# The odd mixer's convolution: one product for each sixteenth of the TensorE array, straight from the gated channels

## The chip, the cores and the metric

The kernel runs on one core of a Trainium2 chip. The metric is the device time in microseconds (us) of one execution. Three runs of the kernel before took 995.54, 997.87 and 1000.76 us, with a median of 997.87 us. The engines are named as in the profile: PE is TensorE's matmul side and PEld its weight loads, DVE is VectorE, ACT is ScalarE, POOL is GpSimd, SP is the queue that issues the loads of the weights.

## The reference, cut to what matters

The program is one inference step of a two-layer decoder trunk for 256 prompt tokens and 8 single sample tokens (264 columns in all). Each layer is a SwiGLU, a mixer and a second SwiGLU, each behind an RMS norm. The change is in layer 1's mixer, the odd one, and there in the depthwise convolution over 31 positions of each of 512 channels:

```
p = h @ w_in                                   # 1024 -> 512 + 512 + 512
a, gt, xp = jnp.split(p, ODD_SPLITS, axis=-1)
glu = a * jax.nn.sigmoid(gt)
gpad = jnp.concatenate([conv_buf, glu], axis=1)
conv = lax.conv_general_dilated(gpad, conv_w[:, None, :], (1,), 'VALID',
                                feature_group_count=CONV_WIDTH) + conv_b
out_c = jax.nn.silu(layernorm(conv, ln_g, ln_b))       # over the 512 channels
pooled = ...                                           # sums of 2, 4, 8 or 16 tokens of xp
out_d = einsum('btgc,gcd->btgd', pooled, pool_w) * pool_scale
y = jnp.concatenate([out_c, out_d], axis=-1) @ w_out
```

The layer norm needs all 512 convolved channels before any of them can go on to `w_out`.

## The kernel before, in words

Everything lies with channels on the 128 partitions and the 264 tokens along the free axis, so the 1024 model channels are 8 tiles. A matmul with a weight matrix is done in three products of 128x128 by 128x264: high part of the weights with high and low part of the activations, low part of the weights with the high part. Weights come in chunks of 8 tiles of 128x128 (`raw`, loaded by SP); ACT makes the high part (`hi`), DVE the low part (`lo`).

The code is a planner: it emits instructions while it keeps an estimated clock of PE, with costs written in the helpers (`quarter` at L319, for example) and small generators that run between the products of the weight matrices when what they need is due. The order it finds is the order in which each engine executes; every engine works through its own instructions in that order and waits on semaphores for the others.

The odd mixer (`odd_mixer`, L1331) runs like this. `odd_in_cols` (L78) lists twelve column blocks of `w_in`: first `POOL_FIRST` (two) of the four pooling blocks, then for each of four channel blocks i its `a` and its gate, then the other pooling blocks. A column block is 24 products on PE (`odin_c`). `evac` (L1450) takes it out of PSUM: DVE scales `a` to `ga`, the gate to `gt`, ACT makes the sigmoid `sg`, and DVE multiplies both into `gp[i]`, the gated channels with 30 zeros ahead of them.

The convolution of block i needs 31 shifted copies of `gp[i]`. Before, `shifts` (L1359) wrote `gp[i]` to DRAM (`gd[i]`, L1362) and read it back four times (L1368) in another layout, `rr`: a group of 32 partitions holds the same 32 channels, shifted by 0, 1, 2 or 3 tokens, and along the free axis stand the four groups of channels. Then `conv` (L1386) ran 8 steps of 4 products, each 128 rows deep and 32 columns wide (L322, `quarter`): the 128 rows are 4 taps of 32 channels, the weights `dg` a diagonal matrix for each tap, and the four products of a step stand in different column groups of the array. The result is one PSUM bank, which ACT takes to `cv[i]` with the bias.

Behind the convolutions follow the steps of the layer norm, each a short exchange of PE with DVE and ACT: `mean` (L1487) gives `mu` (a product with a constant matrix that averages over channels), four subtractions, four squares `csq`, their sum, `cvar`, an inverse square root on DVE (`cvv` to `cv_y`), `cvb` (spread over the partitions), four scalings `cn`, the SiLU `cs`, and the split into `oyh` and `oyl` (the parts `y0` to `y3`). Meanwhile PE runs the output projection `od_o` (`mixer_out`, L793): for six of the eight output blocks first the rows that come from the pooling channels (k = 7, 6, 5, 4), 72 products, then those from the convolution (k = 0 to 3), then the last two blocks. The pooling channels come from `pooled` (L1409, DVE) and `pool_mm` (L1438, a product `pp` on PE, split by ACT and DVE).

`side` (L1560) makes the diagonal matrices `dg` on DVE, beside the two SwiGLUs ahead of the odd mixer.

Of the kernel before, what the change touches and what calls it, by code (L numbers as in the profile page):

```python
# [20 lines left out]
P = 128  # L21
D = 1024
KT = D // P
SEQ = 256
# [50 lines left out]
POOL_FIRST = 2  # L75
# [52 lines left out]
TAPS, QUADS = 31, 8  # L128
WIN = 4 * (QUADS - 1) + SEQ
# [53 lines left out]
def trunk(ctx, tc, a, o):  # L183
# [68 lines left out]
    locks = {"s1": [0.0] * 2, "s2": [0.0], "mm": [0.0] * 4, "rr": [0.0] * 4, "pool": [0.0], "big": [0.0] * 6,   # L252
# [1078 lines left out]
    def odd_mixer(src, next_g, dg):  # L1331
        with ExitStack() as on:
            od, od2, odd = pool(on, "od"), pool(on, "od2", 2), pool(on, "odd", space=DRAM)
            gp = [od.tile([P, 32 + SEQ], F32, name=f"gp{i}") for i in range(4)]
            gd = [odd.tile([P, 32 + SEQ], F32, name=f"gd{i}") for i in range(4)]
# [18 lines left out]
            keep, shifted, pds = {}, {}, {}  # L1354

            TO_DRAM, SHIFT = 3500.0, 10600.0
            late = []

            def shifts(i):  # L1359

                yield from need(f"glu{i}")
                tc.keep_in_program_order(nc.gpsimd.dma_start(gd[i], gp[i]))  # L1362
                t = Clock.now
                yield from acquire("rr")
                yield from until(t + TO_DRAM)
                rr = shifted[i] = od2.tile([P, 4, WIN], F32, tag="rr", name=f"rr{i}", bufs=4)
                for s in range(4):
                    tc.keep_in_program_order(nc.gpsimd.dma_start(  # L1368
                        rr[32 * s:32 * s + 32], gd[i].rearrange("(j c) t -> c j t", c=32)[:, :, s:s + WIN]))
                arrive(rr, t + SHIFT)  # L1370
                produce(f"shift{i}", t + SHIFT)
                produce(f"asked{i}")

            def outputs():

                yield from need("asked3")
                n = 0
                while n < 10:
                    if late:
                        out, src = late.pop(0)  # L1380
                        tc.keep_in_program_order(nc.gpsimd.dma_start(out, src))
                        n += 1
                    else:
                        yield 50.0

            def conv(i):  # L1386

                yield from need(f"shift{i}", "glu_in")
# [10 lines left out]
                release("s2", t)  # L1399
                produce(f"cd{i}", t)  # L1400
# [49 lines left out]
            def evac(ci, ps):  # L1450
                rb = cur["rb"]
                ci -= POOL_FIRST
                if 0 <= ci < 8:
# [7 lines left out]
                    else:  # L1461
# [8 lines left out]
                        if i == 3:  # L1470
                            produce("glu_in")
# [69 lines left out]
            spawn(*[shifts(i) for i in range(4)], outputs(), mean(), *[pool_mm(i) for i in (3, 2, 1, 0)],  # L1541
# [11 lines left out]
    with ExitStack() as on:  # L1553
        dgp = pool(on, "dg")
        cw = dgp.tile([P, 4 * QUADS * 4 + 32], F32, name="cw")
        nc.gpsimd.dma_start(cw, a["convw"])
        n = QUADS * 4
        dg = [dgp.tile([P, QUADS, 4, 32], F32, name=f"dg{i}") for i in range(4)]

        def side():  # L1560

            yield 5000.0
            eye = cw[:, 4 * n:].unsqueeze(1).to_broadcast([P, 16, 32])
            for i in range(4):
                for q in range(0, QUADS, 4):
                    yield 3500.0
                    w = cw[:, i * n + 4 * q:i * n + 4 * q + 16].unsqueeze(2).to_broadcast([P, 16, 32])
                    yield from do("dve", lambda: V.tensor_mul(dg[i][:, q:q + 4].rearrange("p q j c -> p (q j) c"), eye, w))
# [6 lines left out]
        odd_mixer("ff10n", V_NG + 40, dg)  # L1575
# [45 lines left out]
def pack_inputs(inp):  # L1621
# [11 lines left out]
    def cols(v):  # L1633
# [17 lines left out]
    taps = np.zeros((4 * QUADS, 4, 4, 32), np.float32)  # L1651
    taps[:TAPS] = f["od_conv_w"][0].reshape(TAPS, 4, 4, 32)
    taps = taps.reshape(QUADS, 4, 4, 4, 32).transpose(1, 4, 2, 0, 3).reshape(P, 4 * QUADS * 4)
    convw = np.concatenate([taps, np.tile(np.eye(32, dtype=np.float32), (4, 1))], axis=1)
# [15 lines left out]
        "convw": convw,  # L1670
# [46 lines left out]
```

## Time and profile before

| what | value |
|---|---|
| median of three runs | 997.87 us (995.54 to 1000.76) |
| the profiled execution, its own time | 998.99 us |
| span of the profiled execution, first to last instruction | 997.2 us |
| mean granted TensorE clock | 0.995 |
| PE busy | 981.4 us (98%) |
| DVE, ACT, POOL busy | 659.8, 479.0, 41.3 us |
| odd mixer on PE, first product to the first one of the next SwiGLU | 703.45 to 793.23 us |

A profile is one execution. The page gives busy times and shares for the span, the span in 40 slices, and the chain of work that ended last. The trace behind it can be asked for the instructions of an engine in order of time (its timeline), for busy times in given stretches, and for the chain in order of time. A product of 128x264 is listed with some 0.28 us, but such products overlap: the next one starts 0.12 us later. A product of float32 operands stands in the trace as two pairs of a weight load and a matmul.

### The profile page before, as it was taken

How to read it: one execution, taken by the hardware profiler on the slowest of the kernel's cores; microseconds unless marked ns; L12 is line 12 of the kernel's file. 1: busy time of each engine (PE TensorE's matmuls, PEld its weight loads, DVE VectorE, ACT ScalarE, POOL GpSimd, SP SyncE). 2: the span in 40 equal slices, each digit the busy share in tenths (PEclk: the TensorE clock that was granted, in tenths of full speed). 3: DMA queues.
4: the chain of work that ended last, by engine and by line, in shares of the span. 5: the costliest groups of instructions: out<-in, count | busy, mean ns of one | idle time of the engine just before them, and what ended most of it. 6: DMA issues, size and time to landing. Idle time of an engine off the chain costs nothing.

```text
span 997.2 us, 20229 instructions
## 1 busy us (share of the span) xinstructions
PE 981.4 (98%) x8332; PEld 961.0 (96%) x8332; DVE 659.8 (66%) x1081; ACT 479.0 (48%) x718; POOL 41.3 (4%) x99
## 2 busy tenths in 40 slices
PE   9999999999999999999999999999998999999997
PEld 7999999999999999999999999999986999999996
DVE  7766666669889866665666666666863776666552
ACT  6544444465566444444444444444432754444440
POOL 2000000031000000000000000000033000000000
PEclk9999999999999999999999999999998999999999
DMA  7755555562636655555555555555583375555531
GB/s 254 256 188 181 181 189 179 181 218 95 199 125 211 218 189 175 186 176 186 178 174 177 190 181 180 190 177 183 183 250 101 107 226 181 186 185 178 188 107 44
DMA packets 50572, 178.26 MB, mean 179 GB/s; under 512 B 6167, under 2 KB 6632, under 8 KB 50480
## 3 DMA queue, kind: packets, MB, share of 16 engines
q1 hardware_dynamic: 46944, 166.38, 50.6%
q0 software_dynamic: 3248, 10.19, 3.5%
q8 instruction: 65, 1.06, 0.5%
q10 hardware_dynamic: 288, 0.41, 0.1%
q14 instruction: 27, 0.22, 0.1%
HBM read 172.94 MB, written 4.01 MB: 177 GB/s over the span
## 4 chain that ended last, share of the span: by engine, by line
PE 92%; DVE 3%; DMA 2%; issue 1%; POOL 1%; ACT 1%; SPq 0%; DVEq 0%; ACTq 0%; POOLq 0%
PE ff_c L314 50%; PE ff_o L314 26%; PE evin_c L314 6%; PE ev_o L314 2%; PE od_o L314 2%; PE odin_c L314 2%; DMA gd<-gp 1%; POOL rr L1368 1%; PE conv L322 1%; DMA rr<-gd 1%; DMA x<-in_xt 1%; DVE lo L337 1%; PE sc L314 0%; PE ff_pb L314 0%; PE fin_ss L314 0%
## 5 line engine op out<-in xcount | busy, mean ns | idle before, releaser
L337 ACT ACTIVATE hi<-raw 128x1024 fp32r<-128x1024 f32 (+1 forms) x316 | 332.0, 1051 | 405.9 <-PE ff_c L314 229.6
L337 DVE TENSOR_TENSOR lo<-raw,hi 128x1024 fp32r<-128x1024 f32 (+1 forms) x316 | 384.3, 1218 | 161.6 <-ACT hi L337 160.6
L314 PE MATMUL ff_o<-ff_gh,hi 128*128 128x264 f32 x704 | 198.4, 282 | 0.0
L314 PE MATMUL ff_o<-ff_gl,hi 128*128 128x264 f32 x704 | 198.3, 282 | 0.0
L314 PE MATMUL ff_o<-ff_gh,lo 128*128 128x264 f32 x704 | 198.3, 282 | 0.0
L314 PEld LDWEIGHTS ff_o<-ff_gh,hi 128*128 128x128 f32 x704 | 131.9, 187 | 0.0
L314 PEld LDWEIGHTS ff_o<-ff_gh,lo 128*128 128x128 f32 x704 | 131.9, 187 | 0.0
L314 PEld LDWEIGHTS ff_o<-ff_gl,hi 128*128 128x128 f32 x704 | 131.9, 187 | 0.0
L314 PE MATMUL ff_c<-start_xh,lo 128*128 128x264 f32 x352 | 99.5, 283 | 0.4 <-DVE lo L337 0.4
L314 PE MATMUL ff_c<-evn_xh,hi 128*128 128x264 f32 x352 | 99.9, 284 | 0.0
L314 PE MATMUL ff_c<-start_xl,hi 128*128 128x264 f32 x352 | 99.5, 283 | 0.4 <-DVE start_xl L337 0.3
L314 PE MATMUL ff_c<-evn_xl,hi 128*128 128x264 f32 x352 | 99.7, 283 | 0.0
L314 PE MATMUL ff_c<-evn_xh,lo 128*128 128x264 f32 x352 | 99.7, 283 | 0.0
L314 PE MATMUL ff_c<-start_xh,hi 128*128 128x264 f32 x352 | 99.5, 283 | 0.1
L314 PE MATMUL ff_c<-ff01n_xh,hi 128*128 128x264 f32 x352 | 99.2, 282 | 0.0
L314 PE MATMUL ff_c<-odn_xh,hi 128*128 128x264 f32 x352 | 99.1, 282 | 0.0
L314 PE MATMUL ff_c<-ff01n_xl,hi 128*128 128x264 f32 x352 | 98.9, 281 | 0.0
L314 PE MATMUL ff_c<-ff01n_xh,lo 128*128 128x264 f32 x352 | 98.9, 281 | 0.0
L314 PE MATMUL ff_c<-odn_xl,hi 128*128 128x264 f32 x352 | 98.9, 281 | 0.0
L314 PE MATMUL ff_c<-odn_xh,lo 128*128 128x264 f32 x352 | 98.9, 281 | 0.0
L337 DVE TENSOR_TENSOR ff_g<-ff_c,ff_sa 128x264 f32<-128x264 f32 x88 | 38.0, 432 | 58.2 <-PE ff_c L314 58.2
L314 PEld LDWEIGHTS ff_c<-start_xh,lo 128*128 128x128 f32 x352 | 66.0, 187 | 1.2 <-DVE lo L337 1.1
(362 smaller groups left out, 1909.1 us busy)
## 6 DMA issues: line engine op xcount, KB each, us to landing
raw<-in_wts SPq DMA_DIRECT2D x309, 512.0 KB, 3.4
rr<-gd POOLq DMA_DIRECT2D x16, 142.0 KB, 4.7
raw<-in_wts SPq DMA_DIRECT2D x8, 256.0 KB, 5.9
x<-in_xt SPq DMA_DIRECT2D x4, 264.0 KB, 5.7
S<-in_sgla POOLq DMA_DIRECT2D x2, 512.0 KB, 4.7
vb<-vbd POOLq DMA_DIRECT2D x4, 256.0 KB, 5.4
out_gla_s<-S POOLq DMA_DIRECT2D x2, 512.0 KB, 4.5
mat<-in_mats POOLq DMA_DIRECT2D x1, 640.0 KB, 5.9
```

The source lines that it names most:

```text
L314: return pe_run(nc.tensor.matmul(out, lhsT=lhsT, rhs=rhs, start=start, stop=stop), out, lhsT, rhs, cost)
L322: Clock.credit -= pe_run(nc.tensor.matmul(out, lhsT=lhsT, rhs=rhs, start=start, stop=stop), out, lhsT, rhs, cost)
L337: ins = tc.keep_in_program_order(f(*args, **kw))
L1368: tc.keep_in_program_order(nc.gpsimd.dma_start(rr[32 * s:32 * s + 32], gd[i].rearrange("(j c) t -> c j t", c=32)[:, :, s:s + WIN]))
```

## The change

The convolution reads `gp[i]` where it lies. The array is used as 16 blocks of 32 rows by 32 columns. Row group j holds channels 32j to 32j+31 of the block, column group n takes the taps q+n (q = 0, 4, ..., 28); the product for (j, n) has the 32x32 diagonal matrix of one tap as weights and a window of 256 tokens of `gp[i]` that begins at that tap. The planner's cost for one is 29 ns. 31 taps times 4 row groups are 124 products. Each row group writes a PSUM bank of its own (two banks of `conv`, and `convc`, `convd`); the four column groups of a bank hold four partial sums of the same 32 channels. ACT copies the four banks to `rr` (now [128, 4, 256] in SBUF), and four products with a stack of identity matrices (`eye`) add up the partial sums into a bank `cs`, from which ACT adds the bias into `cv[i]`. The copies through DRAM, their 20 DMA issues on POOL's queue and the generator `shifts` are gone; the short outputs no longer wait for them. `POOL_FIRST` becomes 1, so that one more pooling block comes behind the gates.

```diff
-POOL_FIRST = 2
+POOL_FIRST = 1
-TAPS, QUADS = 31, 8
-WIN = 4 * (QUADS - 1) + SEQ
+TAPS = 31
...
+    def sixteenth(out, lhsT, rhs, start, stop):
+
+        Clock.credit -= pe_run(nc.tensor.matmul(out, lhsT=lhsT, rhs=rhs, start=start, stop=stop), out, lhsT, rhs, 29.0)
...
-            def shifts(i):
-
-                yield from need(f"glu{i}")
-                tc.keep_in_program_order(nc.gpsimd.dma_start(gd[i], gp[i]))
-                t = Clock.now
-                yield from acquire("rr")
-                yield from until(t + TO_DRAM)
-                rr = shifted[i] = od2.tile([P, 4, WIN], F32, tag="rr", name=f"rr{i}", bufs=4)
-                for s in range(4):
-                    tc.keep_in_program_order(nc.gpsimd.dma_start(
-                        rr[32 * s:32 * s + 32], gd[i].rearrange("(j c) t -> c j t", c=32)[:, :, s:s + WIN]))
...
             def conv(i):
 
-                yield from need(f"shift{i}", "glu_in")
+
+                yield from need(f"glu{i}")
                 yield from acquire("s2")
-                ps = ps2.tile([P, 1024], F32, tag="s2", name=f"conv{i}")
-                for q in range(QUADS):
-                    for j in range(4):
-                        quarter(ps[32 * j:32 * j + 32, 0:SEQ], dg[i][:, q, j], shifted[i][:, j, 4 * q:4 * q + SEQ],
-                                q == 0, q == QUADS - 1, j)
+                yield from acquire("s1", 2)
+                yield from acquire("rr")
+                yield from slot()
+
+                both = ps2.tile([P, 2, 512], F32, tag="s2", name=f"conv{i}")
+                ps = [both[:, 0], both[:, 1], s1_psum(f"convc{i}"), s1_psum(f"convd{i}")]
+                for q in range(0, TAPS, 4):
+                    for s in range(4):
+                        for j in range(4):
+                            n = (j + s) % 4
+                            if q + n < TAPS:
+                                r = slice(32 * j, 32 * j + 32)
+                                sixteenth(ps[j][32 * n:32 * n + 32, 0:SEQ], dg[i][r, q + n], gp[i][r, q + n:q + n + SEQ],
+                                          q == 0, q + n + 4 >= TAPS)
+                rr = od2.tile([P, 4, SEQ], F32, tag="rr", name=f"rr{i}")
+                t = yield from do("act", lambda: A.copy(rr[:, 2], ps[2][:, 0:SEQ]),
+                                  lambda: A.copy(rr[:, 3], ps[3][:, 0:SEQ]), after=Clock.now)
+                release("s1", t)
+                release("s1", t)
+                t = yield from do("act", lambda: A.copy(rr[:, 0:2], both[:, :, 0:SEQ]))
+                release("s2", t)
+                yield from until(t)
+                yield from acquire("s1")
+                yield from slot()
+                cs = s1_psum(f"cs{i}")
+                for j in range(4):
+                    quarter(cs[32 * j:32 * j + 32, 0:SEQ], eye, rr[:, j], True, True, j)
                 release("rr")
                 acc = cv[i][:, 0:SEQ]
-                t = yield from do("act", lambda: A.activation(acc, ps[:, 0:SEQ], AF.Identity,
+                t = yield from do("act", lambda: A.activation(acc, cs[:, 0:SEQ], AF.Identity,
                                                               bias=vec[:, V_CB + i:V_CB + i + 1]), after=Clock.now)
...
-            spawn(*[shifts(i) for i in range(4)], outputs(), mean(), *[pool_mm(i) for i in (3, 2, 1, 0)],
+            spawn(outputs(), mean(), *[pool_mm(i) for i in (3, 2, 1, 0)],
                   *[conv(i) for i in range(4)])
...
-        dg = [dgp.tile([P, QUADS, 4, 32], F32, name=f"dg{i}") for i in range(4)]
+        dg = [dgp.tile([P, TAPS, 32], F32, name=f"dg{i}") for i in range(4)]
```

PE, where the layer norm's mean is taken, before: the last column block of `w_in` ends, `mu` follows at once, and all of `od_o` stands behind it.

```order
L314 MATMUL odin_c_9603<-ff10n_xh_8894,lo_9381 128x264
L314 MATMUL odin_c_9603<-ff10n_xh_9051,hi_9308 128x264
L314 MATMUL odin_c_9603<-ff10n_xl_9052,hi_9308 128x264
L314 MATMUL odin_c_9603<-ff10n_xh_9051,lo_9381 128x264
L314 MATMUL mu<-cvsum,oneN 128x264
L314 MATMUL mu<-cv_9014,oneN 128x264
L314 MATMUL od_o_9729<-oyh_9032,hi_9343 128x264
L314 MATMUL od_o_9729<-oyl_9033,hi_9343 128x264
```

The same place after the change: the last sum `cs` (four products) and nine products of `od_o` stand ahead of `mu`.

```order
L321 MATMUL cs_10115<-rr_10022,eye 32x256 x4
L313 MATMUL od_o_10121<-oyh_9026,hi_9477 128x264
L313 MATMUL od_o_10121<-oyl_9027,hi_9477 128x264
L313 MATMUL od_o_10121<-oyh_9026,lo_9612 128x264
L313 MATMUL od_o_10121<-oyh_9026,hi_9477 128x264
L313 MATMUL od_o_10121<-oyl_9027,hi_9477 128x264
L313 MATMUL od_o_10121<-oyh_9026,lo_9612 128x264
L313 MATMUL od_o_10129<-oyh_9026,hi_9477 128x264
L313 MATMUL od_o_10129<-oyl_9027,hi_9477 128x264
L313 MATMUL od_o_10129<-oyh_9026,lo_9612 128x264
L313 MATMUL mu<-cvsum,oneN 128x264
L313 MATMUL mu<-cv_9008,oneN 128x264
```

Nine more `od_o` products stand just ahead of this `cs`, so that 18 of the first 72 have moved in front of `mu`. Before, the fourth convolution stood nine `odin_c` products ahead of `mu`; now 30 `odin_c` products lie between it and the first `od_o`.

ACT, around the first convolutions, before: the evacuations `cv` follow the last gate's sigmoid.

```order
L337 ACTIVATE hi_9430<-raw_9321 128x1024
L337 ACTIVATE hi_9468<-raw_9383 128x1024
L337 ACTIVATE sg_9483<-gt_9478 128x264
L337 ACTIVATE cv_9011<-conv_9496,vec 128x256
L337 ACTIVATE cv_9012<-conv_9550,vec 128x256
L337 ACTIVATE hi_9610<-raw_9409 128x1024
```

After: the copies of the first convolution's four banks follow the second gate's sigmoid, ahead of the next high parts.

```order
L340 ACTIVATE sg_9225<-gt_9217 128x264
L340 ACTIVATE hi_9258<-raw_9127 128x1024
L340 ACTIVATE sg_9253<-gt_9251 128x264
L340 COPY rr_9404<-convc_9278 128x256
L340 COPY rr_9404<-convd_9279 128x256
L340 COPY rr_9404<-conv_9277 128x512
L340 ACTIVATE hi_9431<-raw_9140 128x1024
L340 ACTIVATE cv_9005<-cs_9461,vec 128x256
```

What moved: the first convolution now stands between the second and the third gate, and ACT waits for it, with the splits of the weights queued behind.

## Rows read from the trace of the kernel before

**Rows 1.** The page: busy time by engine; chain that ended last, by engine.

```profile
PE 981.4 (98%) x8332; PEld 961.0 (96%) x8332; DVE 659.8 (66%) x1081; ACT 479.0 (48%) x718; POOL 41.3 (4%) x99
...
PE 92%; DVE 3%; DMA 2%; issue 1%; POOL 1%; ACT 1%; SPq 0%; DVEq 0%; ACTq 0%; POOLq 0%
```

**Rows 2.** The chain in order of time, 748 to 763: start, us, what.

```profile
749.21 5.58 DMA rr<-gd
755.52 6.50 PE conv L322 x64
```

**Rows 3.** PE's timeline, 740 to 764: start, us, what, idle before and releaser.

```profile
740.87 0.28 PE L314 MATMUL odin_c<-ff10n_xl,hi 128*128 128x264 f32 x1
740.99 0.28 PE L314 MATMUL odin_c<-ff10n_xh,lo 128*128 128x264 f32 x1
741.27 3.66 PE L322 MATMUL conv<-rr,dg 128*32 128x256 f32 x64
...
745.94 0.28 PE L314 MATMUL odin_c<-ff10n_xh,lo 128*128 128x264 f32 x1
747.56 3.66 PE L322 MATMUL conv<-rr,dg 128*32 128x256 f32 x64 [1.34 <-DMA rr<-gd]
...
752.22 0.28 PE L314 MATMUL odin_c<-ff10n_xh,lo 128*128 128x264 f32 x1
755.52 6.50 PE L322 MATMUL conv<-rr,dg 128*32 128x256 f32 x64 [3.02 <-DMA rr<-gd]
...
763.15 0.60 PE L314 MATMUL mu<-cvsum,oneN 128*128 128x264 f32 x2
```

**Rows 4.** Two stretches: busy us of PE, PEld, DVE, ACT, POOL, granted clock, DMA.

```profile
755.00:760.00 5.00, 4.48 (x44) 2.48 (x48) 0.00 (x0) 0.00 (x0) 1.07 (x2) 0.50 0.29 106
760.00:765.00 5.00, 5.00 (x48) 3.73 (x38) 0.76 (x3) 0.71 (x2) 0.00 (x0) 0.87 0.00 0
```

**Rows 5.** PE's timeline at one round of four column products, even mixer.

```profile
279.85 0.28 PE L314 MATMUL evin_c<-ff00n_xh,lo 128*128 128x264 f32 x1
280.06 0.65 PE L322 MATMUL osum<-osq,mat 128*32 128x264 f32 x8
...
280.87 0.29 PE L314 MATMUL evin_c<-ff00n_xl,hi 128*128 128x264 f32 x1
```

**Rows 6.** The even mixer's 64x64 products alone (tile sc), one stretch.

```profile
228.40:229.40 1.00, 0.95 (x60) 0.95 (x60) 0.00 (x0) 0.00 (x0) 1.00 0.00 0
```

**Rows 7.** ACT's timeline at the odd mixer's start, and at its squares.

```profile
717.70 0.46 ACT L337 ACTIVATE oyh<-pp,vec 128x264 fp32r<-128x264 f32 x1
...
721.10 1.28 ACT L337 ACT_TABLE_LOAD   x1
...
740.06 0.47 ACT L337 ACTIVATE cv<-conv,vec 128x256 f32<-128x256 f32 x1 [3.56 <-PE conv L322]
...
764.76 1.44 ACT L337 ACTIVATE csq<-cv 128x264 f32<-128x264 f32 x4 [2.20 <-DVE cv L337]
```

**Rows 8.** DVE's timeline from the mean to the output projection.

```profile
764.24 1.45 DVE L337 TENSOR_TENSOR cv<-cv,mu 128x264 f32<-128x264 f32 x4 [12.02 <-PE mu L314]
...
767.37 1.24 DVE L337 TENSOR_TENSOR csq<-csq,csq 128x264 f32<-128x264 f32 x3
...
771.58 0.21 DVE L337 TENSOR_SCALAR cvv<-cvar 128x2 f32<-128x2 f32 x2 [1.07 <-PE cvar L314]
...
773.68 0.48 DVE L337 SCALAR_TENSOR_TENSOR oyl<-pp,vec,oyh 128x264 fp32r<-128x264 f32 x1
```

**Rows 9.** PE's timeline in the same stretch.

```profile
770.91 0.63 PE L314 MATMUL cvar<-ones,csq 128*128 128x1 f32 x6
...
774.56 0.92 PE L314 MATMUL cvb<-con,cv_y 128*128 128x128 f32 x6
...
777.96 0.39 PE L314 MATMUL od_o<-oyl,hi 128*128 128x264 f32 x1
```

**Rows 10.** PE's timeline where the two orders part.

```profile
719.95 0.61 PE L314 MATMUL pp<-pd,pw 128*128 128x264 f32 x2
```

More of the change, by code (lines that the diff above doesn't have):

```diff
@@ L249, in trunk @@
     gens, avail = [], {}
-    locks = {"s1": [0.0] * 2, "s2": [0.0], "mm": [0.0] * 4, "rr": [0.0] * 4, "pool": [0.0], "big": [0.0] * 6,
+    locks = {"s1": [0.0] * 2, "s2": [0.0], "mm": [0.0] * 4, "rr": [0.0] * 2, "pool": [0.0], "big": [0.0] * 6,
              "msk": [0.0], "pr": [0.0] * 2}
@@ L1328, in even_mixer, with odd_mixer @@
             mixer_out("ev_out", yh, yl, next_g, "ev")
-    def odd_mixer(src, next_g, dg):
+    def odd_mixer(src, next_g, dg, eye):
         with ExitStack() as on:
-            od, od2, odd = pool(on, "od"), pool(on, "od2", 2), pool(on, "odd", space=DRAM)
+            od, od2 = pool(on, "od"), pool(on, "od2", 2)
             gp = [od.tile([P, 32 + SEQ], F32, name=f"gp{i}") for i in range(4)]
-            gd = [odd.tile([P, 32 + SEQ], F32, name=f"gd{i}") for i in range(4)]
             gs = od.tile([P, 4, NB, 31], F32, name="gs")
@@ L1353, in odd_mixer @@
                 yh[i], yl[i] = part(od, f"oyh{i}"), part(od, f"oyl{i}")
-            keep, shifted, pds = {}, {}, {}
-            TO_DRAM, SHIFT = 3500.0, 10600.0
+            keep, pds = {}, {}
             late = []
-            def shifts(i):
-                yield from need(f"glu{i}")
-                tc.keep_in_program_order(nc.gpsimd.dma_start(gd[i], gp[i]))
-                t = Clock.now
-                yield from acquire("rr")
-                yield from until(t + TO_DRAM)
-                rr = shifted[i] = od2.tile([P, 4, WIN], F32, tag="rr", name=f"rr{i}", bufs=4)
-                for s in range(4):
-                    tc.keep_in_program_order(nc.gpsimd.dma_start(
-                        rr[32 * s:32 * s + 32], gd[i].rearrange("(j c) t -> c j t", c=32)[:, :, s:s + WIN]))
-                arrive(rr, t + SHIFT)
-                produce(f"shift{i}", t + SHIFT)
-                produce(f"asked{i}")
             def outputs():
-                yield from need("asked3")
                 n = 0
@@ L1395, in conv @@
+                yield from slot()
+                cs = s1_psum(f"cs{i}")
+                for j in range(4):
+                    quarter(cs[32 * j:32 * j + 32, 0:SEQ], eye, rr[:, j], True, True, j)
                 release("rr")
                 acc = cv[i][:, 0:SEQ]
-                t = yield from do("act", lambda: A.activation(acc, ps[:, 0:SEQ], AF.Identity,
+                t = yield from do("act", lambda: A.activation(acc, cs[:, 0:SEQ], AF.Identity,
                                                               bias=vec[:, V_CB + i:V_CB + i + 1]), after=Clock.now)
-                release("s2", t)
+                release("s1", t)
@@ L1554, in trunk @@
         dgp = pool(on, "dg")
-        cw = dgp.tile([P, 4 * QUADS * 4 + 32], F32, name="cw")
-        nc.gpsimd.dma_start(cw, a["convw"])
-        n = QUADS * 4
-        dg = [dgp.tile([P, QUADS, 4, 32], F32, name=f"dg{i}") for i in range(4)]
+        eye = dgp.tile([P, 32], F32, name="eye")
+        nc.gpsimd.dma_start(eye, a["eye"])
+        dg = [dgp.tile([P, TAPS, 32], F32, name=f"dg{i}") for i in range(4)]
         def side():
             yield 5000.0
-            eye = cw[:, 4 * n:].unsqueeze(1).to_broadcast([P, 16, 32])
             for i in range(4):
-                for q in range(0, QUADS, 4):
+                for q, n in ((0, 16), (16, TAPS - 16)):
                     yield 3500.0
-                    w = cw[:, i * n + 4 * q:i * n + 4 * q + 16].unsqueeze(2).to_broadcast([P, 16, 32])
-                    yield from do("dve", lambda: V.tensor_mul(dg[i][:, q:q + 4].rearrange("p q j c -> p (q j) c"), eye, w))
+                    w0 = V_CW + TAPS * i + q
+                    w = vec[:, w0:w0 + n].unsqueeze(2).to_broadcast([P, n, 32])
+                    yield from do("dve", lambda: V.tensor_mul(dg[i][:, q:q + n],
+                                                              eye.unsqueeze(1).to_broadcast([P, n, 32]), w))
             produce("diag")
@@ L1574, in trunk @@
         finish("diag")
-        odd_mixer("ff10n", V_NG + 40, dg)
+        odd_mixer("ff10n", V_NG + 40, dg, eye)
     with ExitStack() as on:
@@ L1650, in pack_inputs @@
     sconv[..., :30] = f["state_conv"][0].reshape(NB, 30, 4, P).transpose(3, 2, 0, 1)
[L1651 to L1654, printed above, removed]
     spool = np.zeros((P, 4, NB, 16), np.float32)
@@ L1669, in pack_inputs @@
         "spool": spool,
-        "convw": convw,
+        "eye": np.tile(np.eye(32, dtype=np.float32), (4, 1)),
         "poolw": f["od_pool_w"][0].transpose(1, 0, 2),
```

2 lines of the change are left out of this document (removed).

## The prediction

> **What bounds the kernel now.** I read the page first: PE is busy for 98% of the span and carries 92% of the chain that ended last [rows 1]. So what is taken from DVE, ACT, POOL or the queues is worth nothing by itself; a change pays by what PE executes and by what PE waits for. The 2% of DMA in that chain are here: in order of time it comes to the last convolution through a read of the shifted copies [rows 2]. Next I read PE's timeline around the four convolutions. A convolution takes 3.66 us, and PE enters one without a wait 0.28 us after the product before it, where plain products stand 0.12 us apart. The third starts 1.62 us after the product before it, 1.34 of it idle; the fourth 3.30 us after, 3.02 of it idle; both waits end with `rr`. The fourth then takes 6.50 us instead of 3.66 [rows 3]. The stretches by time say why: the granted clock stands at 0.50 (the 1.2 GHz level) from 755 to 760 and at 0.87 on average from 760 to 765 [rows 4] (behind the stretch and its length come PE, PEld, DVE, ACT and POOL, then the clock). Ahead of that fall PE had been idle for 3 us. So the copies through DRAM cost 1.34 + 3.02 = 4.36 us of waiting and 6.50 - 3.66 = 2.84 us of slow clock, 7.20 us in all. Last I read the steps from `mu` to the first product that uses the convolution's channels, since the change puts other work there: PE takes 777.96 - 763.15 = 14.81 us for them [rows 3, 9].
>
> **The waits go: -7.20 us.** The reads come only after `gp` has gone to DRAM; now nothing lies between `gp` and the product but one semaphore. What is late next? The two orders part where PE now runs its second pooling product, at 719.95 [rows 10]. That one comes later after the change; the next column block starts in its place, and the first convolution 12 products into it: 719.95 + 0.1 + 12 x 0.12 = 721.5. Its `gp` needs the first sigmoid. ACT splits the pooling product until 717.70 + 0.46 = 718.16 and then loads the sigmoid's table, 1.28 us [rows 7]; with 0.4 us for the sigmoid (a square of the same size takes 1.44 / 4) that is 719.9. DVE makes `gp` behind the second gate's scaling, which waits for PE until about 720.2, so at about 721.0: half a microsecond to spare. The other three have several microseconds. I take no wait.
>
> **The convolutions themselves: +0.1 us each, +0.4.** 32 products become 124, but each covers a sixteenth of the array where it covered a quarter. If sixteen stream together, there are 8 rounds as before. No row shows more than four blocks at once, so the bounds: nothing added, if the rounds cost the same (3.66); or the pace of the present convolution for each pair of load and matmul, 3.66 / 64 = 57 ns, times 248 pairs = 14.2 us, 10.5 us more each. Between them stands the even mixer's product of 64 by 64, the only one that splits rows and columns: 60 pairs in 0.95 us, under 16 ns a pair [rows 6], which gives 248 x 15.8 = 3.92 us, 0.26 more. That row is nearest in form, and its pairs are themselves held by the streaming of four blocks, so I take a value below it, 0.1 us, for the later start of the round's last blocks.
>
> **The sums `cs`: +3.12 us.** Four products of 32 columns are one round. The even mixer has one such round, `osum`: from the plain product before it to the second one behind it are 280.87 - 279.85 = 1.02 us, of which two plain steps would be 0.24 [rows 5]. So 0.78 each, change of shape included, and four. Lowest 0.5 (the round with no change of shape), highest 1.0. The copies that feed it are three ACT instructions, 0.47 us like `cv` [rows 7] for two of them and an estimated 0.7 for the double one, in two cases with a sigmoid between: some 2.1 us at most, started 0.4 us after the convolution. PE has 33 plain products, 4.0 us, between the convolution and its sum, and 39 at the last. That cover hides them; ACT a microsecond and a half later would show on PE one for one. Queued behind the waiting copies are the splits of weight chunks; PE needs those two to four chunks later (a chunk is 2.9 us of PE), and DVE makes each low part at least 8 tiles ahead, so I take nothing.
>
> **Nothing:** `dg` is eight DVE products as before, beside the SwiGLUs; 20 issues and their bytes leave POOL and the DMA engines, and beside `rr` nobody on PE waited for those.
>
> **The tail: -0.6 us.** To the mean, like for like, the sum is -7.20 + 0.4 + 3.12 = -3.68. Eighteen products of `od_o` now stand ahead of `mu`, 18 x 0.12 = 2.17 us, so `mu` starts at 763.15 - 3.68 + 2.17 = 761.64. They are missing behind it as cover, and so the steps must be followed. Before, DVE subtracts from 1.09 us after `mu` starts; the squares on ACT begin 0.52 later and take 1.44; then DVE does 1.7 us of other work (a pooling block) before the sums of squares, which end 5.46 us after `mu` [rows 3, 7, 8]. That pooling block now stands ahead of the subtractions, and the sums can end at 1.09 + 0.52 + 1.44 + 0.1 + two of three additions (0.82) = 3.97. One `oyl`, 0.41, brings PE's next `od_o` at 4.4, where its own work would be at 3.9: a wait of 0.5. `cvar` follows three products later, at 4.85. From `cvar` to the next `oyl` is 773.68 + 0.48 - 770.91 = 3.25 us [rows 8, 9], to 8.15, a wait of about 0.9; `cvb` at 8.6; from `cvb` to the convolution's channels 777.96 - 774.56 = 3.40 [rows 9]: 12.0 us after `mu` instead of 14.81. So that product starts at 761.64 + 12.0 = 773.64 instead of 777.96, 4.3 us earlier, and what follows has the same instructions. (Of the 14.81, 2.17 went with the moved products; the remaining 0.6 is the tail's gain.)
>
> **The sum.** -7.20 + 0.4 + 3.12 - 0.6 = -4.3 us. The profiled execution took 998.99 us itself, 1.8 more than its span, which gives 994.7; it lies 1.1 above the median of the runs shown, 997.87, from which it would be 993.6. I predict 994.0.
>
> **Rivals.** *The sixteenths don't run sixteen at a time* (slower). For it: no row shows more than four blocks in flight. Against: the 64x64 products keep under 16 ns a pair with rows and columns split. Its price, if eight run together: 31 steps at the present step's 3.66 / 16 = 0.23 us are 7.1 us, 3.4 more than now on PE, four times 13.7 less the 0.4 counted: 994.7 + 13.3 = 1008. It cancels the gain when a convolution costs 1.1 us more than forecast, 4.9 us or 20 ns a pair. The Trainium skill has a rule that speaks for it: in "TensorE: Matmul & The Clock Gate", section "Wait — 56ns, not 53.3ns?", the distance between starts of matmuls never falls below about 25 ns however small they are. By that rule a convolution would take an estimated 248 x 25 ns = 6.2 us and the kernel about 1004; the trace differs, with its 16 ns a pair [rows 6], though for four blocks. The same page, section "Part 3: Packing small matmuls — row/col tiling", has sixteen 32x32 blocks streaming together at about 4 ns apart; no run here shows it yet, and it would leave the sum as it is.
>
> *The tail keeps its length* (no change). With 14.81 us from `mu` on as before, the convolution's channels come at 761.64 + 14.81 = 776.45, and the gain is 1.5 us: 997.5. For it: DVE's order has two weight splits and two pooling blocks close ahead of the mean, and in-order engines pass a delay on. Against: the 1.7 us that left the chain are plain in the rows.
>
> *The first convolution waits for its channels*, so that the change only moves the wait: if `gp` comes two microseconds after its place, as a late table load would make it, 996.7 (no change). For it the thin margin of 0.5 us; against, that all its steps are short.
>
> **Chances.** The forecast 0.66, with its own range 991 to 997; the sixteenths 0.16; the tail 0.11; the first convolution 0.07. A measurement of this kernel can tell about 0.5%, 5 us, from no change: faster means under 992.9. The forecast, 993.6 by the median, lies just short of that, and half of it (0.33) counts as faster, as the unknown costs fall; the other half and the two rivals of no change are 0.51; the sixteenths give slower, 0.16. For eight in ten the range goes from 990.5 to 1003: some 0.06 lie below and 0.12 above, the heavier part of the first rival.
>
> **What would show it.** PE's timeline after: no idle time with `rr` or any DMA ahead of a convolution, and the clock at 1.00 from 715 to 775. A convolution of about 3.75 us with 248 matmuls; 5 us or more means the first rival. Four rounds `cs` of 0.65 us listed time each. `mu` near 761.6, the convolution's channels near 773.6, the next SwiGLU's first product near 789. An idle stretch before the first convolution, with DVE's `gp` as releaser, means the third rival; `mu` on time and those channels at 776 the second. The prediction is wrong if `mu` starts later than 763, or if PE waits in a place that I have not named.

## The result, and the profile after

| | before | after |
|---|---|---|
| median of 16 runs each, in one comparison | 997.36 us (993.48 to 1000.76) | 1003.62 us (1000.00 to 1007.39) |
| ratio, 95% interval | | 1.0069 [1.0055, 1.0083] |
| the stage: odd mixer, first product to the first of the next SwiGLU (profiled execution) | 89.78 us | 93.80 us |
| a convolution, from the plain product ahead of it to the second behind it, less two plain steps of 0.12 | 3.79, 3.86 undisturbed | 6.29, 6.05, 5.85, 6.06 |

The change made the kernel 0.7% slower: 6.3 us, where I had forecast 3.9 to 4.3 us less. The page answers to [rows 1]: PE is busier, with 768 more pairs of load and matmul, and in the chain DMA falls from 2% to 0% while "issue" stays at 1%.

```profile
PE 985.6 (99%) x9100; PEld 964.6 (97%) x9100; DVE 659.9 (66%) x1081; ACT 483.9 (48%) x730; POOL 30.0 (3%) x79
...
PE 95%; DVE 3%; issue 1%; ACT 0%; DMA 0%; SPq 0%; DVEq 0%; ACTq 0%
```

PE's timeline through the first convolution after (start, duration, what, idle before). It answers to [rows 3]:

```profile
718.26 0.28 PE L313 MATMUL odin_c<-ff10n_xh,lo 128*128 128x264 f32 x1
718.47 0.41 PE L325 MATMUL conv<-gp,dg 32*32 32x256 f32 x2
...
718.71 0.38 PE L325 MATMUL conv<-gp,dg 32*32 32x256 f32 x2
...
718.93 0.59 PE L325 MATMUL conv<-gp,dg 32*32 32x256 f32 x2
719.14 0.40 PE L325 MATMUL convc<-gp,dg 32*32 32x256 f32 x1
...
719.77 0.40 PE L325 MATMUL convc<-gp,dg 32*32 32x256 f32 x1
...
723.30 0.38 PE L325 MATMUL convc<-gp,dg 32*32 32x256 f32 x1
724.02 0.61 PE L325 MATMUL convd<-gp,dg 32*32 32x256 f32 x2 [0.35 <-issue]
724.57 0.39 PE L313 MATMUL odin_c<-ff10n_xh,hi 128*128 128x264 f32 x1
```

No wait stands ahead of it: the first convolution has its channels. The first sixteen products (two matmuls each) stream together, their first matmuls 6.7 ns apart. Of the next round one matmul begins 0.46 us after them, at 718.93, and the others only from 719.12 on. The weight loads show the same: 32 begin in the first 0.13 us, and of the three in the next row the last begins 0.65 us after the first of all:

```profile
718.60 0.10 PEld L325 LDWEIGHTS convd<-gp,dg 32*32 32x32 f32 x1
718.72 0.50 PEld L325 LDWEIGHTS conv<-gp,dg 32*32 32x32 f32 x3
719.13 0.10 PEld L325 LDWEIGHTS convc<-gp,dg 32*32 32x32 f32 x1
```

From then on a round of sixteen takes 0.61 to 0.65 us (719.14 to 719.77), where the stream of 256 columns takes 0.43. Near the end PE starts nothing between 723.30 and 724.02, and no engine or transfer is named: the releaser is "issue". Each of the four convolutions has one such stall. Four stretches, one for each convolution (busy us and counts of PE and PEld, DVE, ACT, POOL, then the granted clock, the DMA engines' share and GB/s):

```profile
718.38:724.67 6.29, 5.94 (x251) 4.00 (x249) 3.29 (x9) 0.42 (x2) 0.89 (x2) 1.00 0.47 146
730.51:736.56 6.05, 5.57 (x251) 3.79 (x249) 1.22 (x1) 0.48 (x1) 0.00 (x0) 1.00 0.42 142
742.37:748.22 5.85, 5.58 (x251) 3.64 (x249) 0.43 (x1) 0.00 (x0) 0.00 (x0) 1.00 0.22 85
754.09:760.15 6.06, 5.93 (x251) 3.95 (x249) 2.63 (x6) 0.14 (x1) 0.00 (x0) 1.00 0.41 145
```

The clock stays at 1.00 where it fell in [rows 4]. So the waits and the slow clock did go; the convolutions cost more. PE's timeline behind them, against [rows 9]:

```profile
765.44 0.64 PE L321 MATMUL cs<-rr,eye 128*32 128x256 f32 x8
767.21 0.61 PE L313 MATMUL mu<-cvsum,oneN 128*128 128x264 f32 x2
...
772.00 0.62 PE L313 MATMUL cvar<-ones,csq 128*128 128x1 f32 x6
...
775.65 0.92 PE L313 MATMUL cvb<-con,cv_y 128*128 128x128 f32 x6
...
779.04 0.39 PE L313 MATMUL od_o<-oyl,hi 128*128 128x264 f32 x1
```

A sum `cs` takes 0.64 us listed, and from `mu` to the convolution's channels it is 779.04 - 767.21 = 11.83 us.

### The profile page after: what moved, and what is told of

Same layout as the page of the kernel before. It is cut to its first block, busy times and chain, and to the rows that moved or that the text cites. A ratio compares the mean times of both kernels' runs of the same rounds, so it can differ in the third digit from the quotient of the medians.

```text
span 998.2 us, 21749 instructions
## 1 busy us (share of the span) xinstructions
PE 985.6 (99%) x9100; PEld 964.6 (97%) x9100; DVE 659.9 (66%) x1081; ACT 483.9 (48%) x730; POOL 30.0 (3%) x79
## 4 chain that ended last, share of the span: by engine, by line
PE 95%; DVE 3%; issue 1%; ACT 0%; DMA 0%; SPq 0%; DVEq 0%; ACTq 0%
PE ff_c L313 50%; PE ff_o L313 25%; PE evin_c L313 6%; PE odin_c L313 4%; PE ev_o L313 2%; PE od_o L313 2%; PE conv L325 1%; PE convc L325 1%; DMA x<-in_xt 0%; PE convd L325 0%; PE sc L313 0%; DVE lo L340 0%; PE ff_pb L313 0%; PE fin_ss L313 0%; PE o L313 0%
```

## The experiments

Three theories of the 2.2 us and more by which a convolution exceeds the forecast. *Window*: sixteen products at most (64 instructions, as each stands in the trace as two pairs) are in flight, and the next starts when the oldest ends. *Supply*: PE runs out of instructions. *Array*: small blocks are slow as such, or collide. The kernels with one execution each (`w128`, `order_n`, `eight`, `taps16`, `split`) are read by the times in their traces; `w128` and `taps16` leave out part of the convolution.

### What sets a round: fewer columns, another order, half the blocks

`w128`, 128 columns in each product:

```diff
-  sixteenth(ps[j][32 * n:32 * n + 32, 0:SEQ], dg[i][r, q + n], gp[i][r, q + n:q + n + SEQ],
+  sixteenth(ps[j][32 * n:32 * n + 32, 0:HALF], dg[i][r, q + n], gp[i][r, q + n:q + n + HALF],
...
```

> The convolution's sixteenth products stream 128 columns instead of 256: it leaves out the second half of the tokens and puts the first half's sums in their place; 124 products a convolution as before. In the changed kernel a convolution takes 5.85 to 6.29 us from the plain product ahead of it to the second one behind it, and its rounds of sixteen products take 0.645 us where 256 columns stream in 0.43. Theory A (the number of instructions sets the time: a fixed distance of about 20 ns between products at PE's front): the rounds stay at 0.5 to 0.65 us and a convolution takes 5.0 to 6.3 us. Theory B (at most sixteen products are in flight, and the next waits until the oldest ends): a round shrinks by the 0.21 us that its stream loses, to about 0.43, and a convolution takes 4.0 to 4.6 us. Theory C (the blocks don't stream side by side, the array sets the time): half, 3.0 to 3.3 us.

A round takes 0.41 us in the mean (the third to the seventh of the first convolution), against 0.62 for the same rounds with 256 columns: 0.21 less, which is what the stream lost, the window theory's number. But a convolution still takes 5.16 to 5.87 us, not the 4.0 to 4.6 that I had for that theory, because the stall grew from 0.50 to 0.85 us to 1.41 to 2.26. Around the second one, PE's timeline:

```profile
732.88 0.29 PE L326 MATMUL conv<-gp,dg 32*32 32x128 f32 x2
735.16 0.29 PE L326 MATMUL convc<-gp,dg 32*32 32x128 f32 x1 [2.00 <-issue]
```

What the faster rounds gain, the stall takes back: the second limit is not the array.

`order_n`, the column groups of a row group one after another:

```diff
-  for s in range(4):
-      for j in range(4):
-          n = (j + s) % 4
+  for j in range(4):
+      for n in range(4):
```

> The sixteen products of a round in another order: the four column groups of one row group after one another, instead of one block of every row group in turn. Theory A and B (front end or window): the rounds stay at 0.645 us, the stage at 93.8 within 0.5 us. Theory D (blocks of a row group or a PSUM bank collide, and the order decides): a round differs by more than 0.1 us, a convolution by more than 0.7 us, and the stage by 3 us or more.

Rounds of 0.61 to 0.65 us, stage 93.71: this other order of the blocks changes nothing.

`eight`, two column groups, sixteen rounds of eight products:

```diff
-  for q in range(0, TAPS, 4):
-      for s in range(4):
+  for q in range(0, TAPS, 2):
+      for s in range(2):
...
-              n = (j + s) % 4
+              n = (j + s) % 2
...
```

> The whole convolution with two column groups instead of four: rounds of eight products, sixteen rounds, still 124 products (248 pairs), and the sum over two partial sums. Theory W (sixteen products in flight at most, and the next begins when the oldest ends): with eight blocks two rounds are in flight, the stream of one covers the delay of the other, and a round takes the stream's time, 0.43 to 0.45 us; a convolution 7.0 to 7.4 us. Rival R (a block can't begin its next product before the last one's sums are in PSUM): a round keeps the 0.645 us of the changed kernel, and a convolution takes 10.2 to 10.6 us. Theory S (supply of instructions): a packet's 256 instructions now last 3.4 us or more, longer than the 2.3 to 2.7 us that a packet takes to be of use, so no idle stretch is left in any of the four.

Two rounds take 0.86 to 0.87 us, so 0.43 each, and the first three convolutions 7.26 to 7.27 us, without a stall. The fourth takes 7.53: it loses 0.27 us near its end, where PE goes on 1.3 us after a packet of instructions that took 1.84 us to come in (the next section has these packets), so what the supply theory had for all four holds for three. PE over the first one; all of its span is busy:

```profile
720.87:728.14 7.27, 7.27 (x251) 5.08 (x250) 3.28 (x9) 0.08 (x2) 0.89 (x2) 1.00 0.40 137
```

With eight blocks a round costs its stream alone; with sixteen it costs 0.2 us more, at either width. That a block must wait for its own last sums (rival R) is out. The window theory gave both numbers beforehand, within 0.02 us.

### The stall: fewer instructions, or a pause between them

`taps16`, only taps 0 to 15 (256 PE instructions a convolution), and `split`, which lets the planner put plain products in the middle:

```diff
-  for q in range(0, TAPS, 4):
+  for q in range(0, 16, 4):
...
```

```diff
   for q in range(0, TAPS, 4):
+      if q == 16:
+          yield from slot()
```

> Only taps 0 to 15: it leaves out taps 16 to 30, so 64 products a convolution instead of 124. Each convolution of the changed kernel holds one idle stretch of 0.50 to 0.85 us for which the trace shows no wait, and the rest runs at 20 ns a pair of load and matmul behind a faster first round. Theory of a supply of instructions (PE runs out of instructions once in some 500 that come faster than they can be brought): with 256 a convolution the idle stretch is gone and a convolution takes 2.7 to 3.0 us. Rival (a stall that belongs to the order of the blocks, once in so many rounds, or to the first round): it stays in two or more of the four, and they take 3.2 to 3.6 us.

> The whole convolution, but the planner may put plain products between its first 64 and its last 60 products. Theory of a supply of instructions: plain products use up instructions four to eight times more slowly, so the second half begins with a store of them and the idle stretches of 0.50 to 0.85 us go; each convolution gains them and pays one more change of shape (0.2 to 0.35 us): the stage from the first product of the odd mixer to the first of the next SwiGLU, 93.8 us in the changed kernel, comes to 92 to 93. Rival (a stall that belongs to the order of the blocks): the idle stretches stay, and the stage takes 94.5 to 95.5 us.

In `taps16` the stalls are gone, and each convolution takes 2.89 us; PE is busy through all of it:

```profile
719.71:722.60 2.89, 2.89 (x131) 1.89 (x129) 2.72 (x9) 0.07 (x1) 0.91 (x2) 1.00 0.38 141
```

In `split` they are gone too, in all eight halves (2.88 to 2.89 and 2.81 to 2.82 us; the two halves of the first convolution):

```profile
718.90:721.80 2.90, 2.90 (x131) 1.90 (x129) 2.73 (x9) 0.07 (x1) 0.91 (x2) 1.00 0.39 149
723.95:726.76 2.81, 2.81 (x123) 1.82 (x121) 1.23 (x1) 0.49 (x1) 0.00 (x0) 1.00 0.53 179
```

So a pause cures it, at 5.71 us a convolution. My number for the stage was wrong, though: 96.01 us instead of 92 to 93. The products in the gaps came from the cover of the tail: 36 products of `od_o` with pooling rows lie between `mu` and the convolution's channels instead of 54 (72 in the kernel before). PE waited there, and then the granted clock was 0.57 in the mean of 778 to 786:

```profile
776.74 1.02 PE L313 MATMUL cvb<-con,cv_y 128*128 128x128 f32 x6 [1.35 <-DVE cv_y L340]
779.74 0.59 PE L313 MATMUL od_o<-oyh,hi 128*128 128x264 f32 x1 [1.97 <-ACT oyh L340]
```

`after_again`, the changed kernel unchanged:

> The changed kernel once more, unchanged, for a second profile. The trace shows that PE's instructions come in packets of 16 KB, and each of the four idle stretches ended 1.3 to 1.4 us after the packet asked for last had come in. Theory S (supply): the stretches stand at the same matmul of each convolution as in the first profile (the 245th, 202nd, 159th, 244th), since they hang on the place of the instructions in the program; each again ends 1.2 to 1.5 us after a packet has come in; their length is 0.4 to 1.0 us. The stage is 93.3 to 94.8 us. Rival (chance, a collision with other transfers): they stand elsewhere or some are missing.

The stalls stood behind the same matmuls (the expectation counts from zero) and lasted 0.88, 0.92, 0.62 and 0.55 us; stage 93.96, ratio in this comparison 1.0090 [1.0061, 1.0119]. The trace shows what they wait for. Queue 8 brings PE's instructions in packets of 16 KB, 71 of them; by the page's 2 x 9100 PE instructions that is 256 in each (in the kernel before 65, for 2 x 8332). In the stretch 721 to 723 of the first profile, ahead of the stall at 723.30:

```profile
q8 instruction: 1, 0.02, 3.9%
```

This one came from 721.34 to 722.60, and PE went on at 724.02. In the 27 stalls of seven profiles (four of the changed kernel, `order_n`, `after_pool2`, `w128`) PE always went on 1.24 to 1.52 us after a packet had come in, 2.2 to 2.7 us after the packet began. At 20 ns a pair the 256 instructions of a packet last 128 x 20 = 2.6 us; with 128 columns (0.41 us a round) 1.6 us. `eight` uses them up in 3.5 us, and plain products in 128 x 0.12 = 15 us. The places say the same: counted from the first matmul of the whole program, all 27 stalls stand 48 to 52 matmuls past a multiple of 128, which is a packet's 128 pairs. The packet that ends a stall began 0.54 to 1.75 us after PE had passed the place 128 matmuls earlier. Two whole convolutions in rounds of sixteen with 256 columns have no such stall, the third of `after_pool2` and the one of `hybrid`, both below; their packets began 0.6 and 0.8 us before that. That a new packet is asked for only about when the one before it comes into use is my reading of these times; the request itself is not an event in the trace.

### The same array work in fewer instructions

`wide`: 32 rows by 128 columns, four taps' matrices side by side; twelve shifted copies line up the four partial sums (four on DVE, eight on ACT), and a 32nd tap is zero:

```diff
-  sixteenth(ps[j][32 * n:32 * n + 32, 0:SEQ], dg[i][r, q + n], gp[i][r, q + n:q + n + SEQ],
+  quarter(ps[j][:, 0:SEQ + 3], dg[i][r, q:q + 4].rearrange("p n c -> p (n c)"),
+          gp[i][r, q:q + SEQ + 3], q == 0, q == 28, j)
...
+  return lambda: eng(dst[32 * n:32 * n + 32], src[32 * n:32 * n + 32, ..., n:n + SEQ])
...
```

> The convolution still reads the gated channels where they lie, with four row groups at once, but a product now covers 32 rows and all 128 columns: the weights are four taps' diagonal matrices side by side, so the four column groups get the same window of 259 tokens and hold sums that still have to be moved by 0 to 3 tokens against each other; twelve copies on DVE and ACT do that on the way to SBUF. 32 products a convolution (64 pairs) instead of 124 (248), the same work for the array. Theory N (the number of instructions is what costs: sixteen products in flight and the supply of instructions): a convolution takes 3.7 to 4.0 us from the plain product ahead to the second one behind, with no idle stretch in it, 2.2 us less than in the changed kernel; the stage, 93.8 there, comes to 84.5 to 87 if the copies (some 2.5 us on each engine) stay behind the 33 plain products ahead of the sum, and the kernel to 4 to 7 us under the kernel before. Rival (blocks of 32 rows are slow as such, or reading four banks in turn): the convolution stays at 5.5 us or more and the stage above 92.

The convolution is as theory N said: 3.90 to 3.91 us, busy throughout, no stall, with the four row groups still side by side:

```profile
720.30:724.20 3.90, 3.90 (x67) 3.26 (x65) 0.71 (x3) 0.07 (x1) 0.38 (x1) 1.00 0.31 118
```

So the count of instructions, not the groups of 32 rows, the four banks or the route without DRAM, made the convolutions slow; that blocks of 32x32 lose nothing as such, `eight` has shown. The stage came only to 91.80, not 84.5 to 87, and the kernel to 1.0039 [1.0016, 1.0063] of before: PE now waits in the output projection (engine, line, waited for: us, times, longest), with half a clock from 765.3 for 3.4 us.

```profile
PE od_o L313 <- DVE oyl L340: 3.7, 3, 1.4
PE od_o L313 <- DVE xs L340: 1.9, 2, 1.0
PE cvb L313 <- DVE cv_y L340: 0.4, 1, 0.4
```

DVE's timeline suggests why: it stands 3.33 us idle ahead of its copies, with the pooling (`xp`) queued behind them.

```profile
755.54 2.79 DVE L340 COPY rr<-conv 32x512 f32<-32x512 f32 x4 [3.33 <-PE convd L321]
758.37 1.23 DVE L340 TENSOR_TENSOR lo<-raw,hi 128x1024 fp32r<-128x1024 f32 x1
759.62 0.42 DVE L340 TENSOR_TENSOR xp<-odin_c,odin_rb 128x256 f32<-128x256 f32 x1
```

`wide_act`, the same with those four copies on ACT:

```diff
-  t = yield from do("dve", *[part_sum(V.tensor_copy, rr[:, 0:2], both, n) for n in range(4)], after=Clock.now)
+  t = yield from do("act", *[part_sum(A.copy, rr[:, 0:2], both, n) for n in range(4)])
```

> The convolution by products of 32 rows and 128 columns again (3.9 us each), with all twelve copies on ACT. In the run before it, DVE had four of them (2.79 us a convolution), waited 3.3 us for each convolution ahead of them with the pooling work queued behind, and PE then waited 6.0 us in od_o and cvb and fell to the slow clock (1.7 us). If that queue is the cause, with the copies on ACT (4.3 us a convolution) DVE's pooling is on time: the waits shrink to 0.5 to 2.5 us, the stage comes to 85 to 88 us and the kernel to 0.994 to 0.998 of the kernel before. Rival (the copies are too long wherever they stand, since ACT's weight splits and the last sum wait for them): the stage stays at 89 to 93 us.

My theory failed: 1.0178 [1.0158, 1.0199], stage 100.49. The convolutions stay at 3.90 us up to the third, but the copies hold ACT for 4.9 us (749.54 to 754.46). The fourth convolution began 13.3 us after the third ended, where the others began 7.8 after, and PE waited 10.8 us. Of that, 3.1 us just ahead of the fourth convolution were still for DVE's pooling (`pd`):

```profile
PE od_o L313 <- ACT rr L340: 4.7, 1, 4.7
PE pp L313 <- DVE pd L340: 3.1, 1, 3.1
PE od_o L313 <- ACT oyh L340: 3.0, 1, 3.0
```

So what held `wide` back stays open.

### The change's two parts, each alone

`before_pool1` and `before_pool0`: the kernel before, with the order of the column blocks alone changed.

```diff
-POOL_FIRST = 2
+POOL_FIRST = 1        # before_pool0: 0
```

> The kernel before with the other part of the change alone: one pooling block ahead of the gates instead of two, so that 24 more plain products lie behind the last gate, 2.9 us, while the copies through DRAM run. If the waits for the copies (1.34 and 3.02 us) are what costs, they shrink by 2.9 us in all or more, the clock does not fall, and with it the 2.84 us of slow clock go: the stage 84 to 87 us, the kernel 3 to 6 us less than before. Rival (the copies are late because of POOL's and DVE's order, and come as much later as the plan moves): the stage stays at 89 to 91 us.

> The same with no pooling block ahead of the gates: 5.8 us more of plain products behind the last gate. If the cover is what counts: no wait for a copy is left, the stage 83 to 86 us, and the kernel 4 to 7 us under the kernel before, unless the pooling's own chain (the sums of tokens on DVE, its product, its splits) now comes too late for the output projection, which would show as PE waiting at od_o for DVE: then 88 to 92 us.

One pooling block less ahead of the gates gave 992.16 us against 997.03, ratio 0.9962 [0.9939, 0.9985], stage 82.73: it beats both kernels. In its one profile three convolutions enter without a wait, the fourth with 1.15 us, and the clock stays at 1.00:

```profile
740.62 3.66 PE L322 MATMUL conv<-rr,dg 128*32 128x256 f32 x64
...
746.71 3.66 PE L322 MATMUL conv<-rr,dg 128*32 128x256 f32 x64 [1.15 <-DMA rr<-gd]
```

With none ahead the gain is gone, 0.9994 [0.9976, 1.0012], stage 86.28. Waits ahead of the convolutions stay, 1.0 us for `rr` and 0.7 for ACT's `hi`, and the clock is at half for 3.4 us from 762.0. The pooling comes late, as feared (the longest wait):

```profile
PE od_o L314 <- DVE oyl L337: 2.3, 1, 2.3
```

`after_pool2`, the new convolution with two blocks ahead (`POOL_FIRST = 2`), and `hybrid`, before with only the fourth convolution by sixteenths:

```diff
-  spawn(*[shifts(i) for i in range(4)], ..., *[conv(i) for i in range(4)])
+  spawn(*[shifts(i) for i in range(3)], ..., *[conv(i) for i in range(3)], conv_direct(3))
...
```

> The change's convolution alone, with two pooling blocks ahead of the gates as in the kernel before. If the parts add up, each by itself: against the kernel before, the waits and the slow clock go (7.2 us), the four convolutions cost 2.2 us more and the four sums 0.8 us each (11.9 us), so the stage comes to 89.8 + 4.7 = 94.5, within 93.5 to 96; against the changed kernel nothing, or up to 2 us more where the tail lacks the 24 plain products. Rival (the place of the pooling blocks decides with the convolution by sixteenths too): 97 us or more, or under 92.

> The kernel before, with the last of the four convolutions alone made by sixteenths; the first three use the shifted copies. By the rows: the wait of 3.02 us and the slow clock's 2.84 us at the fourth convolution go, and one convolution by sixteenths (2.2 us more than a plain one) and one sum (0.8 us) come: 2.9 us less than the kernel before if the third convolution's 1.34 us stay, the stage at 86 to 88 us and the kernel at 0.996 to 0.998 of the kernel before. Rival (the wait moves: the third convolution, or the tail behind the last one, takes the time): the stage stays at 89 to 91 us and the ratio at 0.999 to 1.001.

`after_pool2` took 1.0133 [1.0112, 1.0154], stage 98.64; the parts don't add up: the tail has 36 products of cover as in `split`, with 3.8 us of waits and half a clock from 783.6 for 6.8 us. It bears on the supply: with 24 plain products moved ahead, 48 instructions, the stalls came 24 pairs, 48 instructions, earlier (behind the 222nd, 179th and 221st matmul instead of the 246th, 203rd and 245th). The third convolution had none and took 5.34 us, all busy:

```profile
748.39:753.73 5.34, 5.34 (x251) 3.88 (x249) 0.00 (x0) 0.00 (x0) 0.00 (x0) 1.00 0.37 101
```

`hybrid` took 1.0072 [1.0051, 1.0094], stage 90.14, not my 86 to 88: the waits moved (`od_o` for ACT's `oyh` 3.0 us, for its copy of the sums 1.2), and the clock fell to half for 3.4 us from 782.7. It also reached the odd mixer at 707.5 us, later than all others; I didn't follow that up.

### The rest of the 6.3 us: both kernels again

> The kernel before, unchanged. If the part ahead of the odd mixer is alike in both kernels, its first product lies anywhere from 700 to 704 us, as in the profiles of both so far (703.45; 700.43 and 702.79 of the changed kernel), and the stage takes 89.3 to 90.3 us. If the changed kernel pays 2 us ahead of the stage, this one lies at 700 to 701.5.

> The changed kernel, unchanged: the stage 93.6 to 94.2 us with the four idle stretches at the 245th, 202nd, 159th and 244th matmul. The first product of the odd mixer at 700 to 704 us if that part is alike in both, 702 to 704 if this kernel pays 2 us there.

> The kernel before, unchanged, once more: the first product of the odd mixer at 700 to 704 us if that part is alike in both kernels, at 700 to 701.5 if the changed kernel pays 2 us there; the stage 89.3 to 90.3 us.

> The changed kernel, unchanged, once more: the first product of the odd mixer at 700 to 704 us if that part is alike in both kernels, at 702 to 704 if this kernel pays 2 us there; the stage 93.6 to 94.2 us.

The odd mixer began at 702.8 and 703.6 us in the kernel before, at 704.2 and 704.0 in the changed one; over all profiles the means are 703.3 (three) and 702.9 (four), so no loss ahead of it shows, though single executions lie up to 3.7 us apart there. What varies is the stage, contrary to my expectation: 85.97 and 87.96 us before, 95.21 and 94.70 after. Of the two further profiles of the kernel before, PE at the last convolution, first in one, then in the other:

```profile
753.87 3.66 PE L322 MATMUL conv<-rr,dg 128*32 128x256 f32 x64 [2.68 <-DMA out_conv_p<-gp]
```

```profile
755.17 5.17 PE L322 MATMUL conv<-rr,dg 128*32 128x256 f32 x64 [2.38 <-DMA out_conv_p<-gp]
```

The view names the landing of a short output, but that came later than PE's start; the last read of `rr` landed 0.20 us ahead of that start in both, as in the first profile. In one the clock didn't fall at all, in the other for half as long as in the profile of [rows 3, 4] (3.4 us against 6.8). By the measure of the first table, over 3.79 us a convolution, the waits and the slow clock cost 3.56 and 5.55 us there, against 7.34 in the profile that I forecast from (7.20 by its idle times).

## Why the prediction was wrong

**The convolutions, +0.1 us each: the step that failed.** They cost 2.4 us more each: the sixteen of four profiles took 5.78 to 6.79, 6.21 in the mean, against 3.79 undisturbed. Of that the window is 5.34 - 3.90 = 1.44 us (the one without a stall, against `wide`'s same array work) and the stall 6.21 - 5.34 = 0.87; the remaining 0.1, `wide` against the kernel before, is as large as what I had allowed. My row [rows 6], 15.8 ns a pair, had four blocks in flight and 60 pairs, too few blocks to meet the window and too few instructions to outrun a packet. The break-even of the first rival, 20 ns a pair or 4.9 us, was passed; its mechanism, "not sixteen at a time", is half right: the first sixteen do stream together, but the next sixteen must wait for them. What it had priced, eight at a time, 7.1 us, is close to what `eight` takes, 7.26. Where between eight and sixteen products the loss sets in wasn't measured. Matmuls start 6.7 ns apart at the beginning of a convolution, a round has 0.62 us / 32 = 19 ns a pair, and `taps16` runs at 2.89 / 128 = 23 ns with both changes of shape in it; so no fixed distance of 25 ns is at work. The page "TensorE: Matmul & The Clock Gate" of the Trainium skill, section "Wait — 56ns, not 53.3ns?", whose floor of some 25 ns would have given an estimated 6.2 us, was right in the sum by chance. The same page's table of specifications has a queue of 64 for TensorE, which agrees with sixteen products of four instructions in flight.

**The waits, -7.20 us: right in place, too large in size.** They went as forecast, but the profile showed one execution. Over three profiles they cost (7.34 + 3.56 + 5.55) / 3 = 5.5 us. The rule that I used, the sum against the profiled execution and then the shift to the median, shifts the total but not this term.

**The sums, +3.12: right.** 0.76 to 0.77 us each, four are 3.06; the copies stayed behind the cover and PE waited for none.

**The tail, -0.6: right.** From `mu` to the convolution's channels 11.83 us, forecast 12.0; waits for `oyl` of 0.21 and 0.55 us where I had put 0.5 and 0.9 (4.85 + 3.25 in that working is 8.10, not 8.15, which changes nothing). The first convolution's channels came in time, and of what I put at nothing no wait shows. The sign that I had named came: `mu` started at 767.21, later than 763, though the odd mixer began 3 us earlier.

**The sum again**, with the means of three and four profiles: -5.5 + 4 x 2.42 + 3.06 = +7.2, less the tail, 0.6 to 0.8, is 6.4 to 6.6. The stage went from 87.90 to 94.42 us in the mean, +6.5, and the medians differ by 6.3.

**What I did not ask:** whether the other part of the change would do alone. The copies needed 2.9 us more of plain products behind the last gate, and one number gave them that; against that kernel the new convolution costs 11.7 us of stage (94.42 - 82.73, the latter one profile of an execution 2.5 us under its median); the ratios, 1.0069 and 0.9962, give 10.7.

## What to carry to other kernels

Before a product is cut into blocks, count instructions as well as array time: with these products a convolution of 496 instructions took 6.2 us where 128 for the same array work took 3.9. When a wait for a transfer is to go, first try more work in its cover. Take the size of a wait from several profiles of the kernel; waits of 3.02, 2.38 and 2.68 us ahead of the same convolution were followed by 6.8, 3.4 and 0 us at half clock.

## What the runs showed of the hardware that I had not expected

- Sixteen float32 products of 32x32 stream together, but rounds of sixteen don't overlap: 0.61 to 0.65 us a round for 0.43 of stream, 0.41 for 0.21; with eight blocks 0.43, without loss.
- PE can run out of instructions: stalls of 0.50 to 1.25 us in 496 instructions at 20 ns a pair (1.41 to 2.26 at 13 ns), at places that move with the program by as many instructions as are moved ahead. The Trainium skill, "Runtime: NRT & Kernel Launch", section "Instruction fetch mechanics", has the same blocks of 256 instructions, and takes the cost of crossing into the next one to be mostly hidden; these traces differ, with 0.50 to 2.26 us.
